# The queries' RMS norm moved from the rotated queries into the softmax's exponential, its sums of squares taken as columns

## The chip, the cores and the metric

The kernel runs on one core of a Trainium2 chip. Its time is device microseconds of one execution of the whole program. A run is compared by the median of several executions. The engines are named as in the profile: PE (TensorE matmul), PEld (TensorE weight load, overlapping PE), DVE (VectorE), ACT (ScalarE), POOL (GpSimd) and SP (SyncE, which issues most DMAs). Each engine takes its instructions in program order, and semaphores tie the engines together.

## The reference, cut to what matters

Two layers run over 528 tokens (16 meta tokens and 512 grid tokens) of width 2048. Layer 0 is grouped-query softmax attention with 16 query heads and 8 key/value heads of 128; layer 1 is gated linear attention. The change touches layer 0 alone, and there the norm of the queries and the softmax:

```
def rmsnorm(x, w):
    y = xf * lax.rsqrt(jnp.mean(xf * xf, axis=-1, keepdims=True) + NORM_EPS)
    return (y * w)

def attention_mixer(h, w_in, q_norm, k_norm, w_out, ang_row, ang_col):
    q, k, v, gate = split(h @ w_in)
    q = apply_axial_rope(rmsnorm(q, q_norm), ang_row, ang_col)     # (B, L, 16, 128)
    k = apply_axial_rope(rmsnorm(k, k_norm), ang_row, ang_col)     # (B, L, 8, 128)
    s = einsum(q, k) * 128 ** -0.5
    p = softmax(s);  o = p @ v
    return (o * silu(gate)) @ w_out
```

The norm of a query is one number per query and head. It commutes with the rotation and with the product with the keys, so a score can be multiplied by it as well as the query can.

## The kernel before, in words

**Matmuls.** Activations lie transposed: 128 model features on the partitions, 528 tokens along the row, split into halves of 264 (`HALVES`). An fp32 operand is held as a high and a low part in a rounded fp32 type, and a product is three matmuls (`three`, lines 155 to 157): high weight by high activation, high by low, low by high. `weights` loads 128 x 1024 of raw weights by DMA, ACT casts the high part (line 132), DVE subtracts for the low part (line 133). `project` makes one 128-feature tile of queries, keys or gates: 2 halves x 16 k x 3 matmuls of 264 columns.

**Layer 0.** The program starts with the transposition of x and the first group's key and two queries together (up to about 60 us). Then come gates and values by `project` and by a seven-product scheme (`seven`, lines 241 to 243), up to about 297 us; a generator, `first_group`, finishes the norm and rotation of the first key and two queries beside them. From about 297 to 745 us runs the attention: for each of the eight key/value groups `attention` takes 9 query tiles (four of 128 queries for each of the two heads, and one tile with both heads' 16 meta queries), while PE projects the next group's key and two queries (`qkv`) between them. One group lasts about 57 us.

**A query tile.** `softmax` (line 701 on): PE makes the scores `s` in one PSUM tile of two banks (lines 704 to 706), DVE takes the row maximum `mx` (709), ACT the exponential `pn` with `mx` as its bias and the row sum as a by-product (712). `transposed`: PE transposes `pn` into `pT` and `pTm` (724, 726), ACT casts the high part `ph` (728) and DVE subtracts the low part `pl` (729), and the same for `pmt` (730, 731). `pT` and `pTm` share two PSUM buffers, so the transposition of one tile needs the `pl` and `pmt` of the tile before. `weighted` multiplies `vh`, `vl` with `ph`, `pl` into `o` (744 to 747).

**The norm of keys and queries.** In `qkv`, ACT evacuates each half of a projection with the norm's weight (`qw`, line 307) and its square (`sq`, 308). `rope` then starts the rotation on POOL (DMAs of line 314, products of 315 to 317), splits `sq` into `sh` and `sl` (132, 133), and for each half multiplies them on PE by a matrix of ones (328, 329), which leaves the sum over the 128 features in every partition; DVE adds epsilon (331). At the end `late` takes the inverse root on ACT as logarithm and exponential over 128 x 528 (136, 137), DVE multiplies it into the rotated `qw` (335), and ACT and DVE split the product into `qh`, `ql` or `kh`, `kl`. `first_group` does the same for the first group (lines 537 to 544).

**Order.** Python emits the instructions along a model of PE's time (`Clock`): each matmul advances it, and `clk.after` places the steps of the other engines at a given distance. A scheduler then settles each engine's order by readiness and priority.

```
clk.after(steps[2], late)                       # in rope
A.activation(qw[:, a:b], ps, AF.Copy, scale=wcol)
A.activation(sq[:, a:b], ps, AF.Square)         # in take
```

## Time and profile before

| | |
|---|---|
| median of 3 executions | 1764.85 us (1760.74 to 1764.89) |
| the profiled execution | 1762.9 us, its span 1761.0 us |
| PE busy | 1731.7 us, 98% of the span, 12379 matmuls |
| PEld busy | 1627.5 us, 92% |
| DVE busy | 1148.4 us, 65% |
| ACT busy | 989.8 us, 56% |
| POOL busy | 394.1 us, 22% |
| granted TensorE clock | 0.998 |

A matmul is recorded with its whole latency, about 0.28 us for 264 columns, while the next one starts 0.12 us after it. What a matmul costs PE is therefore read from start to start, not from its length. An idle time that a row shows before a matmul begins only at the modelled end of the one before, so the loss from start to start is about 0.16 us more (0.28 - 0.12).

### The profile page before, as it was taken

The numbers are of one execution on the slowest core, as the hardware profiler recorded it, in microseconds if no ns is written. First come the engines' busy times: TensorE is split into PE (matmuls) and PEld (weight loads), VectorE is DVE, ScalarE is ACT, GpSimd is POOL, SyncE is SP. The second block draws the span as 40 slices with busy tenths as digits, with TensorE's granted clock in tenths as the row PEclk, the third lists the DMA queues.
The fourth block names the chain that finished last, engine by engine and source line by source line (L and its number), as shares of the span: only waits on it lengthen the run. The fifth ranks groups of instructions, "written<-read, shape, count | busy, mean of one in ns | idle before, by whom it ended". The sixth has DMA issues, their size and how long they took to land. (4 is left out here: it accounts for less than half of the span.)

```text
span 1761.0 us, 31489 instructions
## 1 busy us (share of the span) xinstructions
PE 1731.7 (98%) x12379; PEld 1627.5 (92%) x12379; DVE 1148.4 (65%) x1799; ACT 989.8 (56%) x2032; POOL 394.1 (22%) x495
## 2 busy tenths in 40 slices
PE   8999999999999999999999999999999999999998
PEld 8999999999999999999999999998888889888886
DVE  5867776566666666776766976657676776763224
ACT  5545445666666666644457445547677686853222
POOL 3103301355556554241241001110010000000000
PEclk9999999999999999999999999999999999999999
DMA  8444443334334334373485344444333332444323
GB/s 253 140 131 134 127 121 117 85 98 119 101 96 111 99 104 132 121 216 103 133 246 168 115 127 121 123 131 127 93 95 105 94 106 78 126 133 168 95 96 132
DMA packets 273348, 220.99 MB, mean 125 GB/s; under 512 B 13324, under 2 KB 243408, under 8 KB 272672
## 3 DMA queue, kind: packets, MB, share of 16 engines
q1 hardware_dynamic: 253920, 158.76, 31.8%
q0 software_dynamic: 19280, 60.23, 10.5%
q8 instruction: 97, 1.59, 0.4%
q14 instruction: 51, 0.42, 0.1%
HBM read 177.92 MB, written 34.53 MB: 121 GB/s over the span
## 5 line engine op out<-in xcount | busy, mean ns | idle before, releaser
L155 PE MATMUL pp<-uh,whi 128*128 128x264 f32 (+1 forms) x1744 | 549.5, 315 | 0.9 <-POOL whi L384 0.8
L157 PE MATMUL pp<-uh,wlo 128*128 128x264 f32 (+1 forms) x1744 | 538.5, 309 | 1.0 <-DVE wlo L133 0.7
L156 PE MATMUL pp<-ul,whi 128*128 128x264 f32 (+1 forms) x1744 | 538.6, 309 | 0.5 <-DVE ul L446 0.4
L133 DVE TENSOR_TENSOR wlo<-wraw,whi 128x1024 fp32r<-128x1024 f32 (+1 forms) x222 | 276.0, 1244 | 238.1 <-ACT whi L132 234.7
L132 ACT CAST whi<-wraw 128x1024 fp32r<-128x1024 f32 (+1 forms) x222 | 231.3, 1042 | 267.0 <-PE f L1490 83.4
L157 PEld LDWEIGHTS pp<-uh,wlo 128*128 128x128 f32 x1744 | 328.6, 188 | 18.5 <-DVE wlo L133 1.1
L155 PEld LDWEIGHTS pp<-uh,whi 128*128 128x128 f32 x1744 | 328.9, 189 | 17.3 <-POOL whi L384 1.1
L156 PEld LDWEIGHTS pp<-ul,whi 128*128 128x128 f32 x1744 | 329.4, 189 | 14.4 <-DVE ul L446 1.0
L132 ACT CAST whi<-x 128x1024 fp32r<-128x1024 f32 x82 | 86.0, 1049 | 121.2 <-PE pp L242 67.0
L133 DVE TENSOR_TENSOR wlo<-x,whi 128x1024 fp32r<-128x1024 f32 x82 | 102.1, 1253 | 43.3 <-ACT whi L132 43.2
L712 ACT ACTIVATE pn<-s,mx 128x528 f32<-128x528 f32 (+1 forms) x72 | 50.2, 698 | 82.0 <-DVE mx L709 82.0
L241 PE MATMUL px<-uh,whi 128*128 128x264 f32 x320 | 91.2, 285 | 0.0
L243 PE MATMUL px<-uh,wlo 128*128 128x264 f32 x320 | 91.0, 284 | 0.0
L242 PE MATMUL px<-ul,whi 128*128 128x264 f32 x320 | 90.6, 283 | 0.0
L709 DVE TENSOR_REDUCE mx<-s 128x1 f32<-128x528 f32 (+1 forms) x72 | 50.7, 705 | 44.6 <-PE s L706 43.7
L1490 PE MATMUL f<-whi,ul 128*128 128x512 f32 x192 | 75.6, 394 | 0.0
L1488 PE MATMUL f<-whi,uh 128*128 128x512 f32 x192 | 75.5, 393 | 0.0
L1489 PE MATMUL f<-wlo,uh 128*128 128x512 f32 x192 | 75.3, 392 | 0.0
L314 POOL DMA_DIRECT2D qs<-qw x96 | 47.7, 503 | 86.4 <-ACT sq L308 66.7
L242 PEld LDWEIGHTS px<-ul,whi 128*128 128x128 f32 x320 | 60.2, 188 | 0.0
L243 PEld LDWEIGHTS px<-uh,wlo 128*128 128x128 f32 x320 | 60.1, 188 | 0.0
L241 PEld LDWEIGHTS px<-uh,whi 128*128 128x128 f32 x320 | 60.1, 188 | 0.0
(491 smaller groups left out, 4528.6 us busy)
## 6 DMA issues: line engine op xcount, KB each, us to landing
wraw<-in_gla_w_in_dram SPq DMA_DIRECT2D x77, 512.0 KB, 4.0
wraw<-in_attn_w_in_dram SPq DMA_DIRECT2D x75, 512.0 KB, 4.6
wraw<-in_gla_w_out_dram SPq DMA_DIRECT2D x32, 512.0 KB, 3.9
wraw<-in_attn_w_out_dram SPq DMA_DIRECT2D x23, 512.0 KB, 4.6
x<-in_attn_w_in_dram SPq DMA_DIRECT2D x19, 512.0 KB, 4.4
x<-in_gla_w_in_dram SPq DMA_DIRECT2D x19, 512.0 KB, 4.2
qs<-qw POOLq DMA_DIRECT2D x96, 66.0 KB, 4.0
g_d<-y POOLq DMA_DIRECT2D x20, 264.0 KB, 2.4
```

Source lines behind the costliest of these rows:

```text
L132: A.copy(hi, src)
L133: V.tensor_tensor(lo, src, hi.bitcast(F32), op=ALU.subtract)
L155: PE.matmul(ps, wh, uh[:, k, a:b], start=first, stop=False)
L156: PE.matmul(ps, wh, ul[:, k, a:b], start=False, stop=False)
L157: PE.matmul(ps, wl, uh[:, k, a:b], start=False, stop=last)
L241: PE.matmul(ps, w[0][:, k], bh[:, k], start=k == 0 and not more, stop=False, skip_group_check=more)
L242: PE.matmul(ps, w[0][:, k], bl[:, k], start=False, stop=False, skip_group_check=more)
L243: PE.matmul(ps, w[1][:, k], bh[:, k], start=False, stop=k == KH - 1, skip_group_check=more)
L709: V.reduce_max(mx, s, axis=AX.XY, negate=True)
L1488: PE.matmul(ps, uh[:, k, ts], wh[:, kk], start=(k == 0), stop=False)
L1489: PE.matmul(ps, uh[:, k, ts], wl[:, kk], start=False, stop=False)
L1490: PE.matmul(ps, ul[:, k, ts], wh[:, kk], start=False, stop=(k == KT - 1))
```

## The change

A query is no longer multiplied by its inverse root. The rotated `qw`, with the norm's weight but not its scale, is split into `qh` and `ql` at once. The scale is made per query as a column, `f`, and used in the softmax: the negated maximum is multiplied by it on DVE, and the exponential takes it as its per-partition scale.

- The sums of squares no longer come from a matrix of ones. `columns` takes four 128 x 128 pieces of the plain fp32 `sq` as weights and one column of ones as the moving operand: four matmuls of one column for a query head's 512 grid tokens, and for each group's second query a fifth, whose weights are the 16 meta tokens' squares of both heads side by side (32 columns). The key keeps the old way (`rope`).
- `fcs` are two small tiles, 128 x 9, used in turn by the groups: four columns per head and one for the meta queries. The inverse root now runs over 128 x 4 or 128 x 5.
- Epsilon comes as a column too (`ecol`), with one tiny DMA that copies its 16 meta rows.
- `take` puts the second query's last 16 squares into the first query's `sq`, which is 16 columns wider, so its second half takes two squares instead of one.

```
+    def take(wcol, first=None):
+            if first is None or b < T:
+                A.activation(sq[:, a:b], ps, AF.Square)
+            else:
+                A.activation(sq[:, a:SEQ], ps[:, :SEQ - a], AF.Square)
+                A.activation(first[:, T:], ps[:, SEQ - a:], AF.Square)
...
+    def columns(fc, h, ps, sq, metas):
+        for t in range(4):
+            PE.matmul(ps[:, t:t + 1], sq[:, t * P:(t + 1) * P], ones[:, :1], start=True, stop=True)
+        f = fc[:, 4 * h:4 * h + 4 + h]
+        with tc.high_priority(AHEAD):
+            V.scalar_tensor_tensor(f[:, :4], ps[:, :4], 1.0 / P, ecol[:, :4], op0=ALU.mult, op1=ALU.add)
+        if h:
+            PE.matmul(ps[:2 * META, 4:5], metas, ones[:, :1], start=True, stop=True)
+            with tc.high_priority(AHEAD):
+                V.scalar_tensor_tensor(f[:2 * META, 4:], ps[:2 * META, 4:5], 1.0 / P, ecol[:2 * META, 4:],
+                                       op0=ALU.mult, op1=ALU.add)
+        rsqrt_inplace(f)
+
+    def query(h, qw, sq, first, fc, outs, steps):
+        rotate(qw, wk.tile([P, T], F32, tag="qs", name="qs"))
+        def sums():
+            ps = ps_p.tile([P, 512], F32, tag="pp", name="ssc")
+            columns(fc, h, ps, sq, first[:, SEQ:])
+        def late():
+            for hi, lo, a, b in outs:
+                split(hi, lo, qw[:, a:b])
+        clk.after(steps[0], sums)
+        clk.after(steps[1], late)
...
     def first_group():
+        nc.gpsimd.dma_start(out=ecol[META:2 * META, 4:], in_=ecol[:META, 4:])
...
+            if i:
+                yield 7.0
+                columns(fcs[0], i - 1, ps_t.tile([P, 512], F32, tag="t", name="ssc"), sq, metas)
+                yield 7.0
+            for a, b in HALVES if i == 0 else ():
...
     def qkv(g):
-            qw, sq, evac = take(col(KN if i == 0 else QN))
+            qw, sq, evac = take(col(KN if i == 0 else QN), first if i == 2 else None)
             project(w_in0, c, HALVES, evac)
-            rope(qw, sq, outs[i], ((5.0, 9.5, 10.5), (4.6, 9.0, 10.0), (6.5, 10.5, 11.5))[i])
+            if i == 0:
+                rope(qw, sq[:, :T], outs[i], (5.0, 9.5, 10.5))
+            else:
+                first = sq if i == 1 else first
+                query(i - 1, qw, sq, first, fcs[g % 2], outs[i], ((4.6, 10.0), (6.5, 11.5))[i - 1])
...
-    def softmax(n, qh, ql, kh, kl, inv):
+    def softmax(n, qh, ql, kh, kl, f, inv):
         V.reduce_max(mx, s, axis=AX.XY, negate=True)
+        V.tensor_tensor(mx, mx, f, op=ALU.mult)
-        A.activation(pn[:, :T].rearrange("p (a b) -> p a b", a=2), s, AF.Exp, bias=mx, accum_out=sm)
+        A.activation(pn[:, :T].rearrange("p (a b) -> p a b", a=2), s, AF.Exp, bias=mx, scale=f, accum_out=sm)
```

The order on the engines moves at three places that matter. The first is PE at the beginning of a group, after the scores `s` of its first query tile, where the second query's sums stand (`ssq` before, `ssc` now; `pp` is the projection running meanwhile). Before:

```order
L704 MATMUL s<-kh_3244,qh_3246 128x264
L705 MATMUL s<-kh_3244,ql_3247 128x264
L706 MATMUL s<-kl_3245,qh_3246 128x264
L328 MATMUL ssq<-sh,ones_r 128x264
L329 MATMUL ssq<-sl,ones_r 128x264
L155 MATMUL pp<-uh,whi 128x264
L156 MATMUL pp<-ul,whi 128x264
```

Now:

```order
L756 MATMUL s<-kl_3235,qh_3236 128x264
L353 MATMUL ssc<-ones,sq 128x1 x4
L155 MATMUL pp<-uh,whi 128x264
L156 MATMUL pp<-ul,whi 128x264
L157 MATMUL pp<-uh,wlo 128x264
L155 MATMUL pp<-uh,whi 128x264
L156 MATMUL pp<-ul,whi 128x264
L157 MATMUL pp<-uh,wlo 128x264
L155 MATMUL pp<-uh,whi 128x264
L156 MATMUL pp<-ul,whi 128x264
L358 MATMUL ssc<-ones,sq 32x1
L157 MATMUL pp<-uh,wlo 128x264
```

The two sums of the first half became the four columns; the meta columns stand eight matmuls later, and the second pair of sums, some fifty matmuls further on, is gone.

The second place is DVE at the group's second and third query tile, where the second query's split stands (`ql` of 512 and of 16 columns). Before:

```order
L729 TENSOR_TENSOR pl<-pT,ph 128x4x128
L731 TENSOR_TENSOR pmt<-pTm,pmt 32x128
L335 TENSOR_TENSOR qw_98<-qw_98,sq 128x528
L626 SCALAR_TENSOR_TENSOR vm_3269<-vpm,rcol,vm_3269 16x128
L709 TENSOR_REDUCE mx<-s 128x1
L133 TENSOR_TENSOR ql_3243<-qw_98,qh_3242 128x512
L133 TENSOR_TENSOR wlo<-wraw,whi 128x1024
L133 TENSOR_TENSOR ql_3243<-qw_98,qh_3242 128x16
L718 RECIPROCAL rs<-sm 128x1
L729 TENSOR_TENSOR pl<-pT,ph 128x4x128
L133 TENSOR_TENSOR sl<-sq,sh 128x528
L731 TENSOR_TENSOR pmt<-pTm,pmt 32x128
```

Now:

```order
L760 TENSOR_TENSOR mx<-mx,fc_97 128x1
L133 TENSOR_TENSOR ql_3237<-qw_103,qh_3236 128x512
L663 SCALAR_TENSOR_TENSOR vl<-vps,rcol,vh 128x128
L133 TENSOR_TENSOR ql_3237<-qw_103,qh_3236 128x16
L769 RECIPROCAL rs<-sm 128x1
L133 TENSOR_TENSOR wlo<-wraw,whi 128x1024
L780 TENSOR_TENSOR pl<-pT,ph 128x4x128
L782 TENSOR_TENSOR pmt<-pTm,pmt 32x128
L672 SCALAR_TENSOR_TENSOR vm_3263<-vpm,rcol,vm_3263 16x128
L759 TENSOR_REDUCE mx<-s 128x1
L760 TENSOR_TENSOR mx<-mx,fc_97 128x1
L133 TENSOR_TENSOR wlo<-wraw,whi 128x1024
```

The multiplication of `qw` is gone and both pieces of `ql` stand one tile earlier, ahead of the weight split `wlo` and the `pl` that they stood behind; each maximum is followed by its product with `f`. The next rows are `rs`, `pl`, `sl` (now the key's alone) and `pmt`, as before.

The third place is ACT near the end of a group, where the first query's split and a weight cast stand. Before:

```order
L749 COPY o_sb<-o 128x272
L132 CAST qh_3242<-qw_97 128x528
L132 CAST whi<-wraw 128x1024
L307 ACTIVATE qw_98<-pp,cols 128x264
L308 ACTIVATE sq<-pp 128x264
L728 CAST ph<-pT 128x4x128
```

Now:

```order
L800 COPY o_sb<-o 128x272
L132 CAST whi<-wraw 128x1024
L311 ACTIVATE qw_103<-pp,cols 128x264
L315 ACTIVATE sq<-pp 128x248
L316 ACTIVATE sq<-pp 128x16
L779 CAST ph<-pT 128x4x128
```

The cast of `qh` has left this place for one two query tiles earlier, and the square of the evacuation is in two pieces.

More of the change, by code (lines that the diff above doesn't have):

```diff
@@ L777, in attention @@
                 n, c, puts, ends, fresh, i = item
-                pn = softmax(n, qh[:, c:c + n], ql[:, c:c + n], kh, kl, None if last else rs[:, i:i + 1])
+                pn = softmax(n, qh[:, c:c + n], ql[:, c:c + n], kh, kl, fcs[g % 2][:n, i:i + 1],
+                             None if last else rs[:, i:i + 1])
             yield slot / 2
@@ L824, in hybrid_encoder @@
     last_gs = [gate(14)]
-    slots = qws + [vt] + [wk.tile([P, T], F32, tag=tag, name="ogr") for tag in ("qs", "sq")]
+    slots = qws + [vt] + [wk.tile([P, T], F32, tag="qs", name="ogr"),
+                              wk.tile([P, T + META], F32, tag="sq", name="ogr")[:, :T]]
     NS = len(slots)
```

21 lines of the change are left out of this document (14 added, 7 removed).

## The prediction

> **What bounds the kernel now.** I read the page's busy times first, then PE's stretches by stage, then what PE waited for in the stage that the change touches, and last the time lines of DVE, ACT and PE around those waits.
>
> ```profile
> PE 1731.7 (98%) x12379; PEld 1627.5 (92%) x12379; DVE 1148.4 (65%) x1799; ACT 989.8 (56%) x2032; POOL 394.1 (22%) x495
> 297.00:745.00 448.00, 440.25 (x3600) 1.00 0.39 108
> ```
>
> PE is busy for 98% of the span, and for 440.25 of the 448 us of the attention stage (second row: length of the stretch, then PE's busy time). Whatever takes PE's own time is paid in full, and whatever relieves another engine pays only through PE's waits. These are PE's waits of the attention stage, with one from the stage before it (us in total, times, longest):
>
> ```profile
> PE pT L724 <- DVE pl L729: 2.9, 7, 0.9
> PE o L745 <- DVE pl L729: 2.1, 7, 0.4
> PE pTm L726 <- DVE pmt L731: 1.7, 6, 0.3
> PE po L155 <- DVE pl L729: 0.5, 1, 0.5
> PE o L744 <- ACT ph L728: 0.3, 1, 0.3
> ...
> PE pp L243 <- DVE wlo L133: 1.8, 1, 1.8
> ```
>
> The five rows of the attention are 7.5 us in 22 waits. A wait counts from the modelled end of the matmul before, 0.16 us after the next could have started, so the loss is 7.5 + 22 x 0.16 = 11.0 us. That is all that relief of DVE and ACT can give there; the last row, 2.0 us with its tail, lies in the stage that finishes the first queries.
>
> **What PE pays.** Before, each of 16 queries has four sums of 264 columns. In the row of starts below the two sums take 0.25 us up to the next projection, 0.125 each:
>
> ```profile
> 311.17 0.29 PE L328 MATMUL ssq<-sh,ones_r 128*128 128x264 f32 x1
> 311.29 0.29 PE L329 MATMUL ssq<-sl,ones_r 128*128 128x264 f32 x1
> 311.42 0.28 PE L155 MATMUL pp<-uh,whi 128*128 128x264 f32 x1
> ```
>
> So 64 x 0.125 = 8.0 us go. No matmul with one moving column stands in this trace. The nearest is the small plain fp32 product of line 505, which has full 128 x 128 weights and, for its last piece, only 16 moving columns:
>
> ```profile
> L505 PE MATMUL mrow<-dg,ones 128*128 128x16 f32 x2 | 0.3, 222 | 0.0
> ...
> 58.77 0.53 PEld L505 LDWEIGHTS mrow<-dg,ones 128*128 128x128 f32 x4
> 59.22 0.19 PEld L155 LDWEIGHTS pp<-uh,whi 128*128 128x128 f32 x1
> ```
>
> Two things are read here. One fp32 matmul is recorded as two (one piece of 16 columns, x2), each with its own weight load. And four loads, the last two of which belong to the 16-column piece, take 59.22 - 58.77 = 0.45 us up to the next load: 0.1125 each, whether 128 or 16 columns follow. With so few columns the load sets the pace. A column matmul then costs 2 x 0.1125 = 0.225 us, nearly twice the sum of 264 columns that it replaces, and there are as many of them: 64 x 0.225 = 14.4 us. The eight meta products load 32 columns twice. At most they cost a full pair, 8 x 0.225 = 1.8; at least the next projection's load is laid open once, 8 x 0.1125 = 0.9; I take 1.4, since a load of a quarter of the columns should be nearer the lower end. PE's own bill is 14.4 + 1.4 - 8.0 = +7.8 us, and the bounds of the meta products make it 7.3 to 8.2. Where the loads hid under the neighbours entirely it would be -8.0; two rows of 16 columns speak against that, and I keep it as a rival.
>
> [...]
>
> **What DVE and ACT are relieved of, and which waits that ends.** These groups hold the prices:
>
> ```profile
> L331 DVE SCALAR_TENSOR_TENSOR sq<-ssq,erow 128x264 f32<-128x264 f32 x42 | 17.9, 425 | 1.8 <-PE ssq L329 1.3
> L335 DVE TENSOR_TENSOR qw<-qw,sq 128x528 f32<-128x528 f32 x21 | 16.0, 761 | 3.5 <-issue 3.1
> L133 DVE TENSOR_TENSOR sl<-sq,sh 128x528 fp32r<-128x528 f32 x21 | 14.7, 699 | 0.2
> L493 DVE TENSOR_SCALAR cols<-cols 128x1 f32<-128x1 f32 x1 | 0.1, 149 | 0.0
> L136 ACT ACTIVATE sq<-sq 128x528 f32<-128x528 f32 x24 | 15.4, 640 | 4.3 <-DVE sq L539 3.5 <-DVE sq L331 0.8
> L307 ACT ACTIVATE qw<-pp,cols 128x264 f32<-128x264 f32 x42 | 19.8, 471 | 1.3 <-PE pp L157 1.3
> L308 ACT ACTIVATE sq<-pp 128x264 f32<-128x264 f32 x42 | 16.3, 388 | 0.0
> ```
>
> A query loses on DVE 699 + 2 x 425 + 761 = 2.3 us and on ACT three passes like line 136's 0.64. Each of nine tiles of a group gains on DVE a product of one column, bounded by line 493's 0.149 and that plus a bubble of 0.05 for waiting on the maximum just written: take 0.2. On ACT it gains a scale read per partition; 471 against 388 for the same 264 columns with and without such an operand says 0.08. Per group DVE is 2 x 2.3 - 9 x 0.2 - three small additions of about 0.15 = 2.3 us lighter. These are averages; what counts is where the relief falls. One group of the attention, on DVE:
>
> ```profile
> 468.75 1.23 DVE L133 TENSOR_TENSOR wlo<-wraw,whi 128x1024 fp32r<-128x1024 f32 x1 [1.31 <-PE vpm L622]
> ...
> 470.92 0.71 DVE L335 TENSOR_TENSOR qw<-qw,sq 128x528 f32<-128x528 f32 x1
> ...
> 472.66 1.04 DVE L133 TENSOR_TENSOR ql<-qw,qh 128x512 fp32r<-128x512 f32 x1
> 473.62 1.24 DVE L133 TENSOR_TENSOR wlo<-wraw,whi 128x1024 fp32r<-128x1024 f32 x1
> 474.78 1.30 DVE L133 TENSOR_TENSOR ql<-qw,qh 128x16 fp32r<-128x16 f32 x1
> 476.07 0.67 DVE L729 TENSOR_TENSOR pl<-pT,ph 128x512 fp32r<-128x512 f32 x1
> 476.66 0.69 DVE L133 TENSOR_TENSOR sl<-sq,sh 128x528 fp32r<-128x528 f32 x1
> ```
>
> The second query's multiplication (0.71) and both pieces of its split (1.04 and 1.30) stand ahead of the `pl` and `pmt` that PE's next transposition waits for. Now the first is gone and the split stands one tile earlier, ahead of the `wlo` of 468.75, before which DVE idled 1.31 us. DVE should come to the late `pl` some 2 to 3 us sooner. The waits that hang on it:
>
> ```profile
> 420.42 0.66 PE L724 MATMUL pT<-ident,pn 128*128 128x128 f32 x4 [0.79 <-DVE pl L729]
> 534.04 0.65 PE L724 MATMUL pT<-ident,pn 128*128 128x128 f32 x4 [0.30 <-DVE pl L729]
> 590.56 0.66 PE L724 MATMUL pT<-ident,pn 128*128 128x128 f32 x4 [0.26 <-DVE pl L729]
> 647.40 0.66 PE L724 MATMUL pT<-ident,pn 128*128 128x128 f32 x4 [0.19 <-DVE pl L729]
> 699.01 0.66 PE L724 MATMUL pT<-ident,pn 128*128 128x128 f32 x4 [0.86 <-DVE pl L729]
> ...
> 696.53 1.82 DVE L335 TENSOR_TENSOR qw<-qw,sq 128x528 f32<-128x528 f32 x1
> ```
>
> The first four are 1.54 + 4 x 0.16 = 2.2 us, the six of `pTm` 1.7 + 6 x 0.16 = 2.7, and the fifth, behind a multiplication of 1.82 that is gone, 1.0: together 5.9. The other two `pT` waits follow the key's multiplication, which stays. At the end of a group it is ACT that is late:
>
> ```profile
> 510.01 0.63 ACT L132 CAST qh<-qw 128x528 fp32r<-128x528 f32 x1 [0.56 <-DVE qw L335]
> 510.56 1.05 ACT L132 CAST whi<-wraw 128x1024 fp32r<-128x1024 f32 x1
> ...
> 513.64 0.39 PE L745 MATMUL o<-pl,vh 128*128 128x256 f32 x1 [0.35 <-DVE pl L729]
> ```
>
> `qh` waits 0.56 for DVE's multiplication, and behind it on ACT stand `whi` and the evacuation, then the `ph` for which `pl` and `o` wait. With `qh` moved away `whi` starts about 0.55 sooner, more than the 0.35 + 0.16 lost at `o`. The waits at `o` are 2.1 + 0.3 + 8 x 0.16 = 3.7 us; I take 2.5 of them, since `whi` also waits for PE to free its buffer. In all 8.4 of 11.0 us are recovered.
>
> **What is laid on instead.** The product with `f` and the scale lengthen the way from scores to `pn` by 0.2 + 0.08, and ACT's casts queue behind it. In a group's middle there is room, the next scores starting 0.64 us after the end of the exponential that frees their bank:
>
> ```profile
> 473.25 0.69 ACT L712 ACTIVATE pn<-s,mx 128x528 f32<-128x528 f32 x1
> ...
> 474.58 0.28 PE L704 MATMUL s<-kh,qh 128*128 128x264 f32 x1
> ```
>
> The meta product now waits on PE for DVE's addition over the four columns, eight projection matmuls (1.0 us) earlier in the order. DVE has the tile's maximum (0.7) to do while PE makes the columns (0.9), and is free then; if it were late, the whole projection would stand behind. For all of this I take 1.0 us; it lies between nothing and the 2.6 that the waits kept (11.0 - 8.4) already show for DVE's lateness. The epsilon DMA and the two cleared tiles lie at the start, far ahead of their use.
>
> **Sum.** +7.8 - 8.4 + 1.0 = +0.4 us on the profiled execution's 1762.9, so 1763.3. The median shown is 1.95 above that execution; the same step gives 1765.2. Halfway lies 1764.3.
>
> **Rivals.**
> - *DVE's waits stay.* They then hang on the weight split, 1.23 us behind a cast that PE paces, not on the work removed; the moved split would merely make the `pl` one tile earlier late. The columns are paid and nothing comes back: 1762.9 + 7.8 = 1770.7, and 1772.7 by the median's step. It decides once less than 2.5 of the 11.0 us are recovered. For it speaks that a `wlo` stands ahead of every late `pl`; against it the 2 to 3 us taken from that very stretch, and the 1.31 us of idle time where the split goes.
> - *Loads hide.* If the column loads ran under their neighbours, PE's bill would be between -8.0 and, at half the price (7.2 + 0.9 - 8.0), +0.1. With 8.4 recovered and 1.0 laid on that gives 1747 to 1756, in the middle 1751. Against it stands the 0.1125 at 16 columns. [...]
> - *The softmax becomes the chain.* If ACT runs 0.5 us later than now at most tiles, the room of 0.64 is used up by the added 0.28, and each of 72 tiles loses some 0.15: 11 us more than the sum, 1774. The lower load of both engines speaks against it.
>
> **How the numbers follow.** Forecast 0.73, waits stay 0.15, loads hide 0.09, softmax chain 0.03. About 0.3%, 5.3 us, is what can be told from no change here. The forecast's own spread runs from 1757 (all 11.0 us and the 2.0 of the earlier stage come back, nothing laid on: 1762.9 + 7.3 - 13.0) to 1769; of its 0.73 it leaves 0.03 below and 0.02 above the 0.3%. So faster 0.12, same 0.68, slower 0.20. The range takes in the first rival: 1757 to 1773.
>
> **What would show it.** Two loads 0.11 apart per column matmul, and about 0.9 us from its first to the next projection; PE's `pT` and `pTm` waits down from 13 to a few, those at `o` shorter; the exponential near 0.78 us in place of 0.70; DVE's busy time about 20 us lower. Wrong would be column matmuls at 0.05 us each, `pTm` waits still once per group, or new waits of the scores for the exponential.

## The result, and the profile after

The changed kernel takes 1784.59 us (median of 4, 1781.03 to 1786.33) against 1764.87 for the kernel before beside it: a ratio of 1.0114, 95% interval 1.009 to 1.0137. The forecast was 1764.3 and its range ended at 1773. The profiled spans, 1779.2 against 1761.0, differ by 18.2 us (the profiled execution is the fastest of the changed kernel's four), and the two programs can be laid beside each other stage by stage.

The busy time by stage comes first: the stretch, its length, PE's busy time and matmuls, then PEld, DVE, ACT and POOL, then the granted clock, the DMA share and GB/s. Of the kernel before:

```profile
110.00:289.90 179.90, 178.09 (x1453) 177.88 (x1451) 128.43 (x131) 83.53 (x123) 35.19 (x43) 0.99 0.41 121
289.90:738.80 448.90, 440.99 (x3604) 432.50 (x3602) 290.03 (x538) 292.26 (x733) 223.16 (x245) 1.00 0.39 106
```

Of the changed kernel, from the same place to the first scores, and from there to the end of the attention (the last two rows; the first two are short stretches that are read further below):

```profile
204.60:207.80 3.20, 3.20 (x16) 3.20 (x16) 2.40 (x4) 0.42 (x2) 0.00 (x0) 0.53 0.55 164
208.40:211.60 3.20, 3.20 (x28) 3.20 (x28) 1.32 (x2) 1.09 (x2) 0.59 (x1) 1.00 0.21 84
110.00:296.30 186.30, 180.53 (x1461) 180.09 (x1459) 126.77 (x124) 81.17 (x119) 33.95 (x43) 0.98 0.39 117
296.30:756.50 460.20, 449.75 (x3676) 440.67 (x3674) 280.66 (x574) 276.59 (x725) 222.49 (x245) 1.00 0.37 103
```

The stage of the first queries is 6.4 us longer: 4.0 of it is PE's idle time (186.30 - 180.53 = 5.8 against 1.8), 2.4 is busy time. The attention is 11.3 us longer: 8.8 busy and 2.5 idle (10.45 against 7.91). After the attention nothing more than 0.5 us is added. DVE and ACT did become lighter in the attention, by 9 and 16 us, and it brought nothing.

PE's waits from the first queries to the end of the attention in the changed kernel (us, times, longest), then those of its weight loads, where the waits at `o` are now listed, and one row of ACT's:

```profile
PE s L754 <- ACT pn L763: 5.3, 5, 1.4
PE pT L775 <- DVE pl L780: 4.5, 7, 1.1
PE ssc L358 <- DVE fc L356: 2.9, 1, 2.9
PE pp L243 <- DVE wlo L133: 2.8, 1, 2.8
```

```profile
PEld o L796 <- DVE pl L780: 1.7, 7, 0.2
```

```profile
ACT qh L132 <- POOL qw L325: 40.1, 10, 6.2
```

All `pTm` waits are gone, and the same view of the weight loads had `o` at 3.6 us before. In their place the scores wait for the exponential, `pT` waits longer (4.5 against 2.9), and two waits of nearly 3 us stand in the stage of the first queries, where the kernel before has one of 1.8 us.

**Where the softmax chain is late.** The new product of the maximum (count, then shortest, median and longest in ns), and around one long wait of the scores ACT, DVE, POOL and PE:

```profile
L760 DVE TENSOR_TENSOR mx<-mx,fc x72: 147/158/1289, 298.4 to 746.9; 128x1 f32<-128x1 f32 x64, 32x1 f32<-32x1 f32 x8
```

```profile
397.37 0.63 ACT L132 CAST qh<-qw 128x528 fp32r<-128x528 f32 x1 [6.18 <-POOL qw L325]
397.90 0.79 ACT L763 ACTIVATE pn<-s,mx,fc 128x528 f32<-128x528 f32 x1
...
393.87 0.81 DVE L760 TENSOR_TENSOR mx<-mx,fc 128x1 f32<-128x1 f32 x1
...
393.36 1.30 POOL L323 TENSOR_TENSOR qw<-qw,cos 128x528 f32<-128x528 f32 x1 [4.60 <-DMA qs<-qw]
...
398.83 0.39 PE L754 MATMUL s<-kh,qh 128*128 128x264 f32 x1 [1.14 <-ACT pn L763]
```

Two things are seen here. The first query's cast `qh` no longer waits for DVE's multiplication, so the scheduler put it earlier on ACT. There it waits 6.18 us for POOL's rotation, and the exponential, whose maximum was ready at 394.68, stands behind it. This alone makes the wait shown; two more of the five waits of the scores (1.04 and 1.10 us) stand behind such a cast too. And the product itself took 0.81 us in place of 0.16: it ends within 0.02 us of POOL's instruction (393.36 + 1.30 = 394.66). Here this costs nothing, since the cast ends later still, but the longest wait of the scores, 1.40 us at 718.81, stands behind an exponential that waits for a product of 1.02 us and for no cast.

**Where the first queries lose.** DVE, POOL and PE at the first of the two waits, then at the second:

```profile
156.69 4.57 DVE L133 TENSOR_TENSOR wlo<-x,whi 128x1024 fp32r<-128x1024 f32 x2
...
155.64 2.28 POOL L324 TENSOR_TENSOR qs<-qs,sin 128x528 f32<-128x528 f32 x1
...
159.06 0.39 PE L243 MATMUL pp<-t0h,wlo 128*128 128x264 f32 x1 [2.83 <-DVE wlo L133]
...
200.91 2.21 DVE L234 TENSOR_TENSOR wraw<-x,wraw 128x1024 f32<-128x1024 f32 x1
...
204.18 0.15 DVE L356 SCALAR_TENSOR_TENSOR fc<-ssc,ecol 128x4 f32<-128x4 f32 x1
...
204.38 0.22 PE L358 MATMUL ssc<-ones,metas 128*32 128x1 f32 x2 [2.94 <-DVE fc L356]
```

Two weight splits last 4.57 us together where 2.4 is usual, taking turns with POOL's rotation, and PE waits for the second. In the kernel before that rotation stood behind two stores on POOL and then waited 6.59 us for the sums, which held its scratch tile, until 167.93; without those sums it stands ahead of the stores and begins at 148.44. There it meets other weight splits, but it met such splits before as well:

```profile
176.83 4.60 DVE L133 TENSOR_TENSOR wlo<-x,whi 128x1024 fp32r<-128x1024 f32 x2
...
179.23 0.39 PE L243 MATMUL pp<-t0h,wlo 128*128 128x264 f32 x1 [1.81 <-DVE wlo L133]
```

So the collision is not new. What the change adds is 1.0 us at this wait (2.83 against 1.81) and the whole wait of the meta product. That one, near 204 us, waits for DVE's addition, which stands behind DVE instructions lengthened in the same way, such as that of 200.91. And the row 204.60:207.80 above has PE busy throughout with 16 matmuls where the next stretch has 28, at a granted clock of 0.53. So a wait of about 3 us can cost more than itself: half the clock for 3.4 us, some 1.7 us of work. The changed kernel has two such stretches here, from 160.39 and 204.77, the kernel before one, from 180.13.

### The profile page after: what moved, and what is told of

The parts are those of the page before. It is cut to its first block, busy times and chain, and to the rows that moved or that the text cites. A ratio compares the mean times of both kernels' runs of the same rounds, so it can differ in the third digit from the quotient of the medians.

```text
span 1779.2 us, 31632 instructions
## 1 busy us (share of the span) xinstructions
PE 1741.5 (98%) x12459; PEld 1637.7 (92%) x12459; DVE 1136.3 (64%) x1832; ACT 972.1 (55%) x2023; POOL 390.6 (22%) x496
## 4 chain that ended last, share of the span: by engine, by line
PE 76%; DVE 7%; ACT 7%; DMA 4%; issue 2%; POOL 2%; SPq 0%; DVEq 0%; ACTq 0%; POOLq 0%
PE pp L155 10%; PE pp L157 10%; PE pp L156 10%; PE pp L241 4%; PE pp L243 4%; PE pp L242 4%; PE px L241 3%; PE px L243 3%; PE px L242 3%; PE f L1543 2%; PE f L1541 2%; PE f L1542 2%; ACT whi L132 2%; DVE wlo L133 2%; DMA wraw<-in_attn_w_in_dram 1%
## 5 line engine op out<-in xcount | busy, mean ns | idle before, releaser
L763 ACT ACTIVATE pn<-s,mx,fc 128x528 f32<-128x528 f32 (+1 forms) x72 | 56.8, 789 | 56.6 <-DVE mx L760 51.9
L780 DVE TENSOR_TENSOR pl<-pT,ph 128x512 fp32r<-128x512 f32 (+1 forms) x80 | 47.7, 596 | 22.4 <-ACT ph L779 21.9
```

The source lines that it names most:

```text
L763: A.activation(pn[:, :T].rearrange("p (a b) -> p a b", a=2), s, AF.Exp, bias=mx, scale=f, accum_out=sm)
```

## The experiments

All ratios below are to the kernel before, measured on the same chip as the experiment; 0.001 is 1.8 us. The changed kernel stands at 1.0114.

**The meta product ahead of the addition.**

```
 for t in range(4):
     PE.matmul(ps[:, t:t + 1], sq[:, t * P:(t + 1) * P], ones[:, :1], start=True, stop=True)
+if h:
+    PE.matmul(ps[:2 * META, 4:5], metas, ones[:, :1], start=True, stop=True)
 f = fc[:, 4 * h:4 * h + 4 + h]
 ...
-    PE.matmul(ps[:2 * META, 4:5], metas, ones[:, :1], start=True, stop=True)
```

> The meta product is issued right behind the four column products, ahead of DVE's first addition, so that it no longer waits on PE for that addition. Theory (the changed kernel loses 6.7 us before the first scores, most of it at this wait of 2.9 us in the stage of the first queries and at the 3.4 us of halved clock behind it): the first scores start 4 to 5 us earlier than in the changed kernel, near 291.5 us, one of the two stretches at clock 0.5 is gone, and the total falls by 4 to 5 us. Rival 1 (the wait costs only its own length, the halved clock has another cause): 2.9 us, and both stretches stay. Rival 2 (DVE is late in that stage anyway, the next product waits in its place): within 1 us of the changed kernel.

Measured: 1774.27 us, ratio 1.0075 (1.006 to 1.009). The stages of this kernel:

```profile
110.00:291.50 181.50, 177.50 (x1460) 177.06 (x1459) 126.76 (x124) 80.87 (x119) 35.28 (x43) 1.00 0.41 120
291.50:747.20 455.70, 448.58 (x3676) 440.96 (x3674) 274.91 (x574) 277.50 (x725) 217.14 (x245) 1.00 0.37 104
```

The first scores come at 291.5 as foretold, 4.8 us sooner. But only 1.8 us of it is idle time (5.8 to 4.0): the waits for the weight split grew to 4.0 us in two. The rest is the clock, 1.00 in place of 0.98; this time no stretch fell to half, although a wait of 3.2 us stayed. The attention too has 3.3 us less idle time (7.12), which was not expected of this edit, and so the total fell by 6.9 us by the ratios and not by 4 to 5.

**Both casts later on ACT.** Ahead of the split, the casts of the queries are tied to their program order:

```
 for hi, lo, a, b in outs:
-    split(hi, lo, qw[:, a:b])
+    pin(A.copy(hi, qw[:, a:b]))
+    V.tensor_tensor(lo, qw[:, a:b], hi.bitcast(F32), op=ALU.subtract)
```

> The casts of the queries' split are kept in program order on ACT, which puts the first query's cast behind one exponential more, one tile later, when POOL's rotation should be done. Theory (the new waits of the scores come from the cast that waits up to 6.2 us for POOL with the exponential queued behind it): PE's waits of the scores for the exponential fall from 5.3 us to below 1 us, the cast's waits for POOL from 40 us to below 10, and the total falls by 4 to 7 us. Rival (the way from the scores to the exponential is itself too long, by the product of the maximum and the scale per query): the waits of the scores stay above 4 us and the total is within 2 us of the changed kernel.

Measured: 1785.4 us, ratio 1.0138 (1.0123 to 1.0153). The waits of the casts for POOL went as foretold, but the scores still wait 5.9 us for the exponential. DVE and ACT at one of these waits:

```profile
423.22 2.13 DVE L374 TENSOR_TENSOR ql<-qw,qh 128x512 fp32r<-128x512 f32 x2
...
425.75 0.71 DVE L760 TENSOR_REDUCE mx<-s 128x1 f32<-128x528 f32 x1
426.50 0.40 DVE L761 TENSOR_TENSOR mx<-mx,fc 128x1 f32<-128x1 f32 x1
```

```profile
426.94 0.79 ACT L764 ACTIVATE pn<-s,mx,fc 128x528 f32<-128x528 f32 x1 [2.32 <-DVE mx L761]
```

Now the second query's split on DVE stands ahead of the maximum, and this split is itself lengthened: it takes 2.13 us beside a POOL instruction that runs from 423.27 to 425.31. By itself this move only changes who is late.

**The product left out.**

```
 V.reduce_max(mx, s, axis=AX.XY, negate=True)
-V.tensor_tensor(mx, mx, f, op=ALU.mult)
```

> The product of the negated maximum by the factor is left out; the exponential keeps its scale per query, so the output is not the reference's. This takes 64 to 72 one-column products off DVE, and the exponential stands ahead of the key's logarithm again, as in the kernel before. Theory (the product's lateness lets the key's logarithm in front of the exponential, which makes the next transposition late; the waits of the scores have another cause, the cast ahead of the exponential): PE's waits at pT fall from about 5.8 us to about 4, those of the scores stay above 4 us, the total falls by 1 to 3 us. Rival (the softmax has become the chain, so its length decides): each of 72 tiles gets 0.15 to 0.25 us back, the total falls by 7 us or more, and the waits of the scores go.

Measured: 1787.41 us, ratio 1.0149 (1.013 to 1.0169). The clause on the output was mistaken: what is subtracted per query cancels in a softmax, so the unscaled maximum leaves the result as it is. PE's waits, and one row of ACT's:

```profile
PE vpm L668 <- DVE vl L663: 11.5, 6, 2.2
PE s L754 <- ACT pn L762: 1.5, 2, 0.8
PE pT L774 <- DVE pl L779: 0.6, 1, 0.6
```

```profile
ACT qh L132 <- POOL qw L325: 49.5, 14, 5.9
```

Both the scores' waits (5.3 to 1.5) and those at `pT` (4.5 to 0.6) went, more than either theory said. But with other lengths the scheduler made another order: the second query's cast now stands in front of the copies `vh` of the values and waits for POOL, and PE waits about 2 us per group at `vpm`. So neither the total nor the waits that went can be put down to the product alone; the run of the scalar form below can say more.

**The columns doubled.**

```
-PE.matmul(ps[:, t:t + 1], sq[...], ones[:, :1], start=True, stop=True)
+PE.matmul(ps[:, t:t + 1], sq[...], ones[:, :1], start=True, stop=False)
+PE.matmul(ps[:, t:t + 1], sq[...], ones[:, :1], start=False, stop=True)
```

> Each of the 64 column products is made twice into the same sum, so the factor comes out smaller by about 1/sqrt(2) and the output is not the reference's; 64 more one-column products, 128 more weight loads, nothing else. Theory (a column product costs its two loads, 0.225 us): the total rises by 14.4 us, 13 to 16 with waits. Rival 1 (all of the changed kernel's 18 us and the 8 us of the old sums are the columns' own price): 64 x 0.4 = 26 us. Rival 2 (the loads hide under their neighbours and all of the loss is waits): below 7 us.

Measured: 1799.36 us, ratio 1.0219 (1.0198 to 1.024), 18.5 us above the changed kernel by the ratios, give or take some 6. The weight loads of a query's columns in the changed kernel, then here:

```profile
353.41 0.98 PEld L353 LDWEIGHTS ssc<-ones,sq 128*128 128x128 f32 x8
354.31 0.19 PEld L155 LDWEIGHTS pp<-uh,whi 128*128 128x128 f32 x1
```

```profile
339.07 0.31 PEld L353 LDWEIGHTS ssc<-ones,sq 128*128 128x128 f32 x2
...
340.87 0.19 PEld L155 LDWEIGHTS pp<-uh,whi 128*128 128x128 f32 x1
```

Eight loads take 0.90 us up to the next projection, sixteen 1.80: 0.1125 each, the predicted price. That is 14.4 us for 64 more products. The profiled execution also has two more stretches at half clock, 6.8 us that do the work of 3.4, which would make most of the other 4 us and which the expectation had not allowed for. The rival of 26 us, 0.4 per product, falls by these rows.

**The product as tensor by scalar.**

```
-V.tensor_tensor(mx, mx, f, op=ALU.mult)
+V.tensor_scalar(mx, mx, f, None, op0=ALU.mult)
```

> The product of the maximum by the factor is the same one-column product in the same place of every queue, but written as a tensor by a scalar per partition instead of a tensor by a tensor. In the changed kernel 27 of its 72 executions begin while POOL runs a two-operand instruction; their median is 0.61 us against 0.15 for the others, and most end within 0.02 us of POOL's instruction. Theory (a DVE instruction with two operands in SBUF and POOL's shut each other out for a whole instruction; one with a single tensor operand isn't shut out): no product above 0.25 us, 11 us of its 22 gone, PE's waits of the scores and of pT fall from 12.3 us to 7 to 10, the total falls by 2 to 5 us. Rival 1 (the scalar is a second SBUF operand and is shut out alike): the same long products, the same time. Rival 2 (the product is not what the tiles wait for, the order of the queues is): the products get short, the waits stay above 11 us and the total is within 1.5 us of the changed kernel.

Measured: 1776.03 us, ratio 1.0081 (1.0066 to 1.0096). The product, PE's waits and the attention's stretch:

```profile
L760 DVE TENSOR_SCALAR mx<-mx,fc x72: 201/206/216, 297.7 to 741.2; 128x1 f32<-128x1 f32 x64, 32x1 f32<-32x1 f32 x8
```

```profile
PE s L754 <- ACT pn L763: 3.4, 5, 1.0
...
PE pT L775 <- DVE pl L780: 1.7, 3, 1.1
```

```profile
295.60:750.90 455.30, 449.46 (x3677) 440.86 (x3675) 274.33 (x575) 276.88 (x725) 221.57 (x245) 1.00 0.37 104
```

Every queue has the same order as in the changed kernel, but for one query tile near 721 us, and only the form of one instruction is other. In the tensor form 27 of 72 products began while POOL ran a two-operand instruction; 18 of them lasted over 0.25 us, and each of these 18 ended 9 to 23 ns after POOL's. In the scalar form 27 began so as well, and none is longer than 216 ns. PE's idle time in the attention falls from 10.45 to 5.84 us, and the total by 5.8 us by the ratios, whose intervals just overlap. The theory held; a shade of the gain goes back in the usual product, 0.206 against 0.158. How sure the size of the gain is will be seen further below, where another kernel with the tensor form has an idle time of 7.07.

**The first query's cast alone later.** As in the run of both casts, with the order kept for `h == 0` only.

> Only the first query's cast stands one tile later on ACT; the second query's, which the run of both had moved too, stays where the changed kernel has it. In the run of both the scores' waits moved to the tile in which DVE had the second query's split (2.13 us) ahead of the maximum. Theory (the first query's cast, waiting for POOL with the exponential behind it, makes the long waits of the scores): the waits of the scores fall from 6.5 to below 3 us and the total falls by 2 to 6 us. Rival (any place of the split blocks someone, and the waits only move): PE's waits in the attention stay at 13 to 16 us and the total is within 2 us of the changed kernel.

Measured: 1782.0 us, ratio 1.0115 (1.0098 to 1.0132). PE's waits in the attention:

```profile
PE pT L778 <- DVE pl L783: 5.2, 7, 1.1
PE s L757 <- ACT pn L766: 2.8, 3, 1.5
```

The scores' waits are halved, the others grow, PE's idle time in the attention falls only from 10.45 to 9.8 us, and the total is where it was: the rival. With the long product in place, neither of the two moves of casts pays.

**The product in the kernel before.**

```
 V.reduce_max(mx, s, axis=AX.XY, negate=True)
+V.tensor_tensor(mx, mx, ones[:n, :1], op=ALU.mult)
```

> The kernel before, with its norm of the queries untouched, and one thing added: the negated maximum is multiplied by a column of ones, tensor by tensor, ahead of the exponential. The output stays the reference's. As in the changed kernel the scheduler now lets the key's logarithm go in front of one exponential of a group. Theory (the product's shut-out by POOL and that order make a good part of the new waits, with no column product and no moved cast): the total rises by 2 to 6 us over the kernel before, some products last as long as a POOL instruction, and waits of the scores or longer ones at pT appear. Rival (the product is harmless by itself, the moved cast and the columns make the loss): within 1.5 us of the kernel before.

Measured: 1768.4 us, ratio 1.0034 (1.0022 to 1.0045), so 6 us for a product whose median is 0.16 us, together with the order that the scheduler made for it:

```profile
L710 DVE TENSOR_TENSOR mx<-mx,ones x72: 147/160/1489, 289.7 to 732.6; 128x1 f32<-128x1 f32 x64, 32x1 f32<-32x1 f32 x8
```

```profile
PE pT L725 <- DVE pl L730: 4.8, 13, 0.5
PE o L746 <- DVE pl L730: 3.8, 8, 1.7
PE s L704 <- ACT pn L713: 2.4, 4, 1.0
```

Here 19 products are lengthened, waits of the scores appear, and those at `pT` rise from 2.9 to 4.8, with no column product and the queries' norm in its old form. But ACT and DVE do not have the order of the kernel before: some hundred instructions on ACT and some thirty on DVE changed places. How the 6 us divide between the long products and that order is not shown.

**Three mends together**: the meta product first, the scalar product, the first query's cast later.

> The changed kernel with three mends: the meta product ahead of DVE's first addition, the product of the maximum as tensor by scalar, the first query's cast one tile later. Theory: what is left over the kernel before are the columns themselves, 8 us, less what of the waits of 12 us is won back: PE's waits in the attention fall from 14.3 to 6 to 9 us, and the total is 1 to 6 us above the kernel before. Rival (the waits only move from place to place): PE's waits in the attention stay above 11 us and the total is no lower than with the meta product alone, 12 us above the kernel before.

Measured: 1770.51 us, ratio 1.005 (1.0031 to 1.0069), 9 us over the kernel before and so above the 1 to 6 expected, and 4.4 us under the meta product alone, with intervals that overlap. PE's idle time in the attention is 4.75 us (451.70 less 446.95), about 7 from start to start, which is the theory. What was not foreseen is that the stage of the first queries still had waits of 3.5 us at the weight split and a stretch at half clock.

**One load per column.** On top of the three mends the squares are written in the rounded type, and two equal columns of ones are moved (shortened):

```
-A.activation(sq[:, a:b], ps, AF.Square)
+A.activation(sq.bitcast(F32R)[:, a:b], ps, AF.Square)
...
-PE.matmul(ps[:, t:t + 1], sq[...], ones[:, :1], start=True, stop=True)
+PE.matmul(ps[:, 2*t:2*t + 2], sq[...].bitcast(F32R), ones_r[:, :2], start=True, stop=True)
```

> The three mends, and the column products in one pass: the squares are written in the rounded fp32r type, so each column product loads its weights once, not twice, and moves two equal columns of ones. Theory (a column product costs its weight loads, 0.1125 us each): 64 loads and 8 meta loads less, 7.2 + 0.9 = 8 us under the three mends, within 3 us of the kernel before; a query's four products take about 0.45 us on PE, and both weight loads of one product become one. Rival (the price is a fixed one per product, of starting it or of its column write): the total falls by less than 3 us.

Measured: 1764.08 us, ratio 1.0014 (1.0004 to 1.0024), 6.3 us under the three mends. A query's loads:

```profile
328.78 0.54 PEld L356 LDWEIGHTS ssc<-ones_r,sq 128*128 128x128 f32 x4
329.24 0.19 PEld L155 LDWEIGHTS pp<-uh,whi 128*128 128x128 f32 x1
```

Four loads, 0.46 us up to the next projection. The price of a column product is that of its loads. The total fell by less than the 8 us expected; in the profiled execution two stretches at half clock fell into the attention, which the three mends do not have there.

**The key later as well.** The steps of `rope` for the key go from (5.0, 9.5, 10.5) to (5.0, 11.0, 12.0).

> As the single pass, and the key's sums and its split come 1.5 us later in the order of steps, so that the key's logarithm no longer stands ahead of an exponential. Theory (that order makes the remaining waits at pT): PE's waits at pT below 1 us, 1 to 2 us under the single pass. Rival (with the product short the order no longer matters): within 1 us of the single pass.

Measured: 1762.25 us, ratio 0.9996 (0.9985 to 1.0007). The waits at `pT` fall from 1.9 to 1.4 us, not below 1, and the intervals overlap. Whether this order matters once the product is short stays unclear.

**No columns at all**, on top of the three mends:

```
 def columns(fc, h, ps, sq, metas):
-    ...
+    return
```

> The three mends, with the column products, the additions and the inverse roots of the queries left out and the factor held at one, so the output is not the reference's. What is left is what the change takes away. Theory: 64 x 0.225 + 8 x 0.26 = 16.5 us under the three mends, about 8 us under the kernel before; PE's waits in the attention as with the three mends, 6 to 8 us. Rival (the columns' place makes waits of its own, at DVE's additions and on ACT): more than 19 us under the three mends.

Measured: 1785.9 us, ratio 1.0137 (1.0124 to 1.015). It was to be 16.5 us under the three mends and is 15 above, with less work on PE, DVE and ACT. ACT and PE in one group:

```profile
414.52 0.62 ACT L363 CAST qh<-qw 128x512 fp32r<-128x512 f32 x1 [5.99 <-POOL qw L325]
```

```profile
419.09 0.28 PE L661 MATMUL vpm<-ident,vt 128*16 128x128 f32 x1 [2.74 <-DVE vl L656]
```

The inverse roots had kept the second query's cast back on ACT. Without them it moved ahead of the exponential's copy, the gate's logarithms and the values' copies, and waited there for POOL. PE waits at `pTm` and `vpm` in six of the seven groups that project the next one, all waits of the attention are 29.5 us from start to start, and six stretches at half clock stand among them.

**No columns, both casts tied.**

> As the run without columns, but both queries' casts keep their program order on ACT; the column products, additions and inverse roots are left out and the factor is held at one, so the output is not the reference's. Theory (without columns the second query's cast slid in front of the values' copies, the exponential's copy and the gates, and waited up to 6.0 us there for POOL; that and the halved clock behind each wait made 32 us): PE's waits in the attention fall from 29.5 to 7 to 12 us, at most two stretches at half clock are left in it, and the total is 1750 to 1758, 12 to 20 us under the three mends. Rival (PE's column products gave the other engines time that they now lack): the waits stay above 20 us.

Measured: 1758.4 us, ratio 0.9976 (0.9964 to 0.9988): 13 us under the three mends, and 28 under the same kernel with the second query's cast left to the scheduler. No stretch of the attention is at half clock. PE's waits there are 13.3 us, a little above the 7 to 12 expected. So the cast's place did it, and the whole of what the change takes away is worth some 4 us to this kernel as it is ordered.

**The rotations of the first queries later.** One more edit to the changed kernel alone: the DMAs of POOL's rotation keep their program order for the two first queries, behind two stores.

```
-nc.gpsimd.dma_start(out=qs[...], in_=qw[...])
+keep(nc.gpsimd.dma_start(out=qs[...], in_=qw[...]))     # keep is pin in first_group for i > 0
```

> The changed kernel with one edit: POOL's rotations of the two first queries keep their place in program order, behind two more stores, as POOL had them in the kernel before. In the changed kernel the first query's rotation begins 20 us earlier, at 154 us, where DVE splits weights, and DVE's weight split there lasts twice 2.3 us in place of 1.2. Theory (that rotation, by shutting DVE out, makes PE's wait of 2.8 us at 159 us, and with it the halved clock behind it): the wait at 159 us is gone, first scores 2 to 4 us earlier than in the changed kernel (292 to 294.5 us), the total 2 to 4 us lower; the meta product's wait near 204 us may stay. Rival (DVE is late there by its own work, or the rotation shuts DVE out in its new place as well): first scores within 1.5 us of 296.

Measured: 1770.46 us, ratio 1.0042 (1.0027 to 1.0057). The two weight splits that took 4.57 us, and the stages:

```profile
154.40 2.35 DVE L133 TENSOR_TENSOR wlo<-x,whi 128x1024 fp32r<-128x1024 f32 x2
```

```profile
110.00:287.00 177.00, 176.83 (x1458) 176.60 (x1457) 122.81 (x124) 81.09 (x119) 34.67 (x43) 1.00 0.41 123
287.00:743.70 456.70, 449.63 (x3676) 440.68 (x3674) 279.95 (x574) 276.74 (x725) 219.47 (x245) 1.00 0.37 104
```

The total is 12.7 us under the changed kernel by the ratios, the most that any single edit brings. The first scores come at 287.0, 9.3 us sooner, more than twice what was expected, and 2.9 us sooner than in the kernel before: 5.6 us of idle time (5.8 to 0.2) and two stretches at half clock (3.4 us) are gone, the wait of the meta product with them. On every engine but POOL the order is that of the changed kernel, on POOL only the rotations of the first queries have another place, and yet the attention's idle time is 7.07 against 10.45 us. So two profiles of one order differ by some 3 us there, and that much of any one profile's attention says nothing of its edit. It may be how POOL's and DVE's instructions happen to meet, but the lengthened products are nearly the same sum in both (10.8 us over the usual 0.158 in the changed kernel, 10.0 here), so the cause is not shown. Against 7.07 the scalar form's 5.84 is a gain of 1.2 us, against 10.45 one of 4.6.

**All mends together**: the single pass with the key later and the rotations later, with the first cast or both tied:

> The single pass with the key later, and the rotations of the first queries later as in the run that moves them alone. Theory: what is gained there comes on top, PE's wait near 159 us and its halved clock go, and the total falls 2 to 4 us under the single pass with the key later, to 0.998 of the kernel before. Rival (the wait moves to another product of that stage): the ratio stays between 0.999 and 1.001.

> As the one before, with both queries' casts in program order on ACT, not the first one's alone. In the run of both casts the scores then waited, because DVE had the second split of 2.13 us ahead of the maximum. Theory (the second split's place decides): PE's waits of the scores are 2 us or more above the run with the first cast alone, the total 1 to 4 us higher. Rival (with the product short there is room for it): within 1 us.

Measured: 1754.68 us, ratio 0.9952 (0.994 to 0.9964), and 1753.36 us, ratio 0.9948 (0.9933 to 0.9964). The first is better than expected, and the second is not the slower one: with the product short there is room for the second split, the rival. The stages of the second:

```profile
110.00:287.00 177.00, 177.00 (x1460) 177.00 (x1460) 124.08 (x124) 81.06 (x119) 34.75 (x43) 1.00 0.41 123
287.00:727.80 440.80, 439.46 (x3614) 432.99 (x3612) 271.17 (x575) 274.99 (x726) 220.70 (x245) 1.00 0.39 107
```

PE has 1.3 us of idle time left in the attention. So the changed kernel does come out 9 us ahead, once its columns load once, one instruction has another form and four places of the order are mended. How much of this is the idea's own is not shown: the kernel before has waits of its own, among them the collision at 176.83 with its stretch at half clock, and no run gave it a later rotation or another such mend. Of the 11.1 us between the profiled spans, 2.9 lie in the stage of the first queries.

## Why the prediction was wrong

**PE's own bill was nearly right.** A query's columns cost 0.90 us, as predicted. The meta pair was to cost 0.175 and at most 0.225; it costs 0.35, by the starts of the projections around it (355.28, 355.64 and 355.87 us, where they are usually 0.12 apart). Right behind the columns, as in the run that moved it there, it costs 0.23. So the bill is 14.4 + 2.8 - 8.0 = 9.2 in place of 7.8. In the attention PE's busy time rose by 8.8 us.

**The recovered waits were right in two of three places.** Those at `pTm` (2.7) are gone, and at `o` 2.3 us from start to start came back of the 2.5 taken. At `pT`, where 3.2 were to come back, waits rose instead. The relief of DVE was real, since with the product in scalar form the waits at `pT` are 1.7 us against 2.9 before, and with all mends 0.5; the same change filled it with something late. DVE's busy time shows it too: it was to fall by about 20 us and fell by 12.1 (1148.4 to 1136.3), and the lengthened products hold the 10.8 us already named.

**The failed step is "what is laid on instead: 1.0 us".** Against it stand 5.3 us of new waits at the scores, 1.6 more at `pT`, and the 6.4 us of the first queries. Three parts of that step failed.

- *The product's price.* "a product of one column, bounded by line 493's 0.149 ... take 0.2" took the row of an instruction with one tensor operand for one with two. Its median is indeed 0.158, and it starts 0.035 us after the end of the maximum, where 0.05 was taken, but 18 of 72 last until a POOL instruction ends, up to 1.29 us, and they stand between the scores and the exponential. The changed kernel with the product in scalar form is some 6 us faster by the ratios, whose intervals just overlap; the kernel before with the product, and with the order that came with it, is 6 us slower. The prediction's own fences had such rows, the multiplication of 1.82 us at 696.53 where its group's mean is 0.76, and a subtraction of only 16 columns that takes 1.30 us at 474.78. POOL ran until 697.80 and 476.04 there. The prediction read both as work that is gone or moved, without asking why they were long.
- *The moved cast.* "With `qh` moved away `whi` starts about 0.55 sooner" looked at the place that the first query's cast left. The place that it went to stands in front of an exponential, at a time when POOL's rotation was not yet done: 40.1 us of waits in 10 casts, of which the first query's seven waited 4.7 to 6.2 us each. What waits behind the moved instruction was worked out for its old place and not for the new one. That POOL became the last thing the cast waits for was not seen.
- *The stage of the first queries.* It was counted only as 2.0 us that might come back, without asking what that wait came from, though it was the same collision of a rotation with weight splits. And the meta product's wait was ruled out by "DVE ... is free then". In the attention that held, where the meta product has no such wait. In the stage of the first queries DVE was not free: the rotations had lost what kept them back and moved forward onto other weight splits, and each of the two waits that followed brought 3.4 us at half clock, one such stretch more than in the kernel before. Of the prediction's error of 17.8 us (18.2 between the profiled spans less the 0.4 of its sum) this stage makes 5 to 6.

**The rivals.** The sign named as wrong, new waits of the scores for the exponential, is what appeared, and "the softmax becomes the chain" (0.03) had the right place. Its price, 0.15 us at each of 72 tiles, had the wrong form: most tiles lose nothing, a few lose over 1 us. No rival was a collision of DVE with POOL, though the two edits that take one away, the later rotations and the scalar product, won 12.7 and some 6 us, and the range could not hold the result without it.

**What stays open.** PE's busy time in the attention rose by 8.8 us, and its columns and meta products there account for 8.0 (12.6 + 2.4 - 7.0); the rest isn't placed. And since the attention's idle time varies by some 3 us between kernels of one order, how the 2.5 us more of idle time there divide between the cast and the product was not settled: the moved casts alone left it at 9.8 us or more, the scalar product alone brought it to 5.84, both with the meta product first to 4.75.

## What to carry to other kernels

Where a step is taken away, look at what it was holding back: an instruction that now comes earlier waits at the head of its in-order queue for its next-latest input, and everything behind it waits too, as the exponential did behind a cast that waited 6.18 us for POOL. Price a small instruction on a critical chain by its longest execution and by what it shares with other engines, not by its median, and prefer a form with one tensor operand in SBUF where POOL works beside it: the longest product took 0.216 us in that form, and 1.289 in the changed kernel's form with two. A wait of 2 us or more on PE should be counted with the slow clock after it: 24 of the 30 such waits in these runs were followed by a stretch at half clock, which costs some 1.7 us of work.

## What the runs showed of the hardware

**DVE and POOL lengthen each other's instructions.** Of the changed kernel's 72 products, with two tensor operands in SBUF, 24 began while POOL ran a two-operand instruction with 0.14 us or more to go, and all 24 ended 9 to 23 ns after it. The other way round POOL's product of 1.3 us takes 2.3 beside DVE's weight split (155.64). The `pl` subtraction, with one operand in PSUM, never exceeds 0.693 us, though 15 of 80 began so, and the form with a scalar per partition never exceeds 0.216. What in the chip makes them wait for each other is not shown.

**Half clock after a wait.** Each of the changed kernel's two waits of 2.8 and 2.9 us was followed by a stretch of 3.4 us at a granted clock of 0.5, in which matmuls start 0.22 us apart in place of 0.12. In each of the 17 traces the clock changes only at the steps of one regular grid, 3.413 us apart. Between 100 and 1500 us, every interval of that grid at full clock in which PE stood idle for 1.8 us or more, 24 of them, is followed by one at half clock (in the kernel before one with 1.81 us, in the changed kernel two with 2.08 and 2.94 us); of 49 intervals with 1.2 to 1.8 us of idle time 4 are. So where a wait falls on the grid matters as well as its length. The kernel with the meta product first agrees, whose wait of 3.2 us brought no such stretch: the grid divides it into 1.5 and 1.7 us.

**A product of one column costs its weight loads**: 0.225 us in fp32, where it is loaded twice (eight loads in 0.90 us), 0.115 in the rounded type, where it is loaded once (four in 0.46).
